# One core: FFN gate and up as one Winograd-Strassen block product, the hidden activation split in the down stage

## The chip, the cores and the metric

The kernel runs on one core of a Trainium2 chip. The metric is the device time of one execution in microseconds (us); the times below are of three runs, and the profile is of one execution more.

## The reference

One transformer-like block over 512 tokens of width 1024: layer norm 0, an input projection, a gated-MLP branch and an HGRN2 branch, a gated merge, an output projection with layer norm 1, a feed-forward part with a per-layer-embedding (PLE) gate, and layer norm 2. What the change touches, with `D_FF` = 2816:

```python
mix = jnp.einsum("bsd,de->bse", merged, w_o[i])
h1 = _layer_norm(ALPHA * h + mix, ln1_g[i], ln1_b[i])
hid = jax.nn.silu(jnp.einsum("bsd,df->bsf", h1, w_ffn_gate[i])) * jnp.einsum("bsd,df->bsf", h1, w_ffn_up[i])
ffn = jnp.einsum("bsf,fd->bsd", hid, w_ffn_down[i])
ple = (jax.nn.sigmoid(jnp.einsum("bsd,de->bse", h1, w_ple_gate[i]) + b_ple_gate[i])
       * jnp.einsum("bsr,rd->bsd", p[i], w_ple[i]))
h = _layer_norm(ALPHA * h1 + ffn + ple, ln2_g[i], ln2_b[i])
```

All inputs are float32, and the result is held to float32 accuracy.

## The kernel before, in words

Every large product is done in float32r from operands that are split in two: `split` (L59) makes the high part h with a cast on ACT (L61) and the low part l with a subtraction (L64), on DVE unless `eng` names another engine. A product is then three matmuls per tile: h by h, h by l, l by h. Weights come from DRAM in units of 512 KB through `load_unit` (L66): SP issues the transfer into a `raw` tile (three buffers), ACT and DVE make `wh` and `wl` (five buffers each).

`gemm_a` (L84) puts features on partitions: the 128x128 weight tile is stationary and the activation, 512 tokens, streams; 48 matmuls with 512 columns for 256 features over K = 1024. `mm_b` (L96) puts tokens on partitions.

The stages are written one after another: PLE product and layer norm 0, HGRN2 by pairs of heads, gated MLP, merge, output projection with layer norm 1 (`ps_wo`; tiles `r1`, `h1h`, `h1l`), PLE gate (`ps_pg`), then the FFN. `turn` (L696) transposes a normed token tile on PE and splits it into `h1h` and `h1l`, straight from PSUM. In the PLE gate a token tile's result goes DVE (add bias, `sgp`), ACT (sigmoid), POOL (times `pl`), DVE (into `r1`).

The FFN loop (L740 on) runs over 11 units m of 256 hidden features. Each unit is two `gemm_a`, `fg` (gate) and `fu` (up), so 96 matmuls and four weight units. Then ACT takes silu from PSUM, DVE multiplies (`fhf`, L753), and `split` makes `hidh` and `hidl` at once. The down stage (`ps_d`) runs over 11 pairs of hidden tiles, and ends with layer norm 2 and the stores.

A scheduler sets the order of each engine's queue when the program is built, from this text and its own estimates; each engine works its queue in that order. Tiles live in pools. A tile placed where an earlier pool lay may be written when the earlier tiles there are done with, and such a wait can stand on any queue, SP's included. PSUM has four tiles of two banks (`ps_tile`).

Of the kernel before, what the change touches and what calls it, by code (L numbers as in the profile page):

```python
# [31 lines left out]
def block_kernel(  # L32
# [155 lines left out]
    with tc.tile_pool(name="start", bufs=1) as sp:  # L188
# [188 lines left out]
    def keys(m, psf):  # L377
        """forget gates, their products, decayed keys"""
# [31 lines left out]
        fl = lambda ap: ap.rearrange("p g c -> p (g c)")  # noqa: E731  # L410
# [56 lines left out]
    def scores(m):  # L467
        """scores, [s, t] of each block of 128 tokens; states at the starts of blocks 1..3"""
# [33 lines left out]
    def outputs(m):  # L502
        """tokens on partitions, normed"""
# [56 lines left out]
    # =============== gated MLP: v, normed; the last pair of heads beside it ===============  # L560
# [13 lines left out]
    # blocks of 64 positions: a later one is not seen from an earlier one  # L574
# [62 lines left out]
    # =============== merge ===============  # L637
# [22 lines left out]
    # =============== output projection, layer norm 1, PLE gate ===============  # L660
# [4 lines left out]
    h1h = h1pool.tile([P, KT, T], F32R, name="h1h")  # L665
    h1l = h1pool.tile([P, KT, T], F32R, name="h1l")
    with tc.tile_pool(name="l1", bufs=1) as lp:
# [4 lines left out]
        g1 = load_bc(lp, ln1_g[0], "g1")  # L672
        b1 = load_bc(lp, ln1_b[0], "b1")
        bpg = load_bc(lp, b_ple_gate[0], "bpg")
        # the residual: alpha * layer norm 0
        for t in range(TT):
# [3 lines left out]
            V.scalar_tensor_tensor(out=r1[:, t, :], in0=xr, scalar=mr0[:, t, 1:2], in1=b0a, op0=ALU.mult, op1=ALU.add)  # L680
        acc = [ps_tile(f"ps_wo{t}") for t in range(TT)]
# [14 lines left out]
        def turn(t):  # L696
# [20 lines left out]
        yapool_cm.__exit__(None, None, None)  # L717
        for c in range(2):
# [20 lines left out]
    # =============== FFN ===============  # L739
    with tc.tile_pool(name="hid", bufs=1, side="right") as fp:  # L740
        hidh = fp.tile([P, FT, T], F32R, name="hidh")
        hidl = fp.tile([P, FT, T], F32R, name="hidl")
        for m in range(FT // 2):
            psg = ps_tile(f"ps_fg{m}")
            gemm_a(psg, wg, 256 * m, h1h, h1l, f"fg{m}")
            psu = ps_tile(f"ps_fu{m}")
            gemm_a(psu, wu, 256 * m, h1h, h1l, f"fu{m}")
            for a in range(2):
                f = 2 * m + a
                sg = fp.tile([P, T], F32, tag="fsg", name=f"fsg{f}", bufs=2)  # L750
                S.activation(sg, psg[:, a, :], AF.Silu)
                hf = fp.tile([P, T], F32, tag="fhf", name=f"fhf{f}", bufs=2)
                V.tensor_tensor(out=hf, in0=psu[:, a, :], in1=sg, op=ALU.mult)  # L753
                split(hidh[:, f, :], hidl[:, f, :], hf)
        h1pool_cm.__exit__(None, None, None)

        with tc.tile_pool(name="fin", bufs=1) as lp:
# [15 lines left out]
            tails = [(kp, [unit_b(wd, 2 * kp, 512 * c, f"d{kp}_{c}", pool=lp, bufs=4) for c in range(2)])  # L773
                     for kp in range(NP - TAIL, NP)]
            for t in range(TT):
# [52 lines left out]
```

## Time and profile before

| | |
|---|---|
| median of 3 runs | 997.42 us (996.73 to 997.47) |
| span of the profiled execution, first to last instruction | 992.0 us |
| output projection's wait to first gate matmul | about 571 to 577 us |
| PLE gate | about 577 to 623.5 us |
| FFN gate and up, first `ps_fg` to first `ps_d` | 623.54 to 862.90 us |
| down stage, layer norm 2, stores | 862.90 to 992.0 us |

PE is the matmul engine, PEld its weight load, DVE the vector engine, ACT the scalar engine, POOL the GpSimd, SP the engine that issues transfers. [...] A wait belongs to the instruction that stood still; the chain follows the work that ended last back to its start.

### The profile page before, as it was taken

The page shows a single profiled execution, that of the slowest core. Times are in us where ns is not written, and L with a number is a line of the kernel's source. Part 1 is how long each engine was busy: PE and PEld are TensorE (multiplying, and loading weights), DVE is VectorE, ACT ScalarE, POOL GpSimd, SP SyncE. Part 2 cuts the span into 40 slices and gives each one's busy share as a digit, 9 for nine tenths or more (in the row PEclk, how much of TensorE's full clock was granted, in tenths as well). Part 3 has the DMA queues.
Part 4 walks back from the last instruction along what each step waited for, and adds up shares of the span by engine and source line. Part 5 has one row for each costly group of instructions (what it writes and reads, how often), then busy time and mean ns, then how long its engine had stood idle before and what let it go on. Part 6 is the DMA issues. An engine that isn't in the chain of part 4 may idle for free.

```text
span 992.0 us, 11393 instructions
## 1 busy us (share of the span) xinstructions
PE 963.9 (97%) x4745; PEld 795.3 (80%) x4745; DVE 474.0 (48%) x538; ACT 289.6 (29%) x335; POOL 132.0 (13%) x106
## 2 busy tenths in 40 slices
PE   6999999998999999999999989999999999999996
PEld 5788878787888888888888868888888888888885
DVE  6667935767249543332324984333323333311307
ACT  4244222333324332232322222332223223212301
POOL 5314410505006000000000332000000000000004
PEclk9999999999999999999999999999999999999999
DMA  8343223225222423333235425333332333322302
GB/s 288 127 138 107 65 81 90 64 65 167 66 65 85 128 77 94 95 97 102 89 106 216 166 81 153 98 93 103 89 106 87 104 90 101 132 102 85 128 1 85
DMA packets 79939, 104.60 MB, mean 105 GB/s; under 512 B 3368, under 2 KB 60304, under 8 KB 79888
## 3 DMA queue, kind: packets, MB, share of 16 engines
q1 hardware_dynamic: 79888, 103.88, 33.4%
q8 instruction: 37, 0.61, 0.3%
q14 instruction: 14, 0.11, 0.0%
HBM read 99.67 MB, written 4.19 MB: 105 GB/s over the span
## 4 chain that ended last, share of the span: by engine, by line
PE 84%; DVE 9%; POOL 2%; DMA 2%; issue 1%; ACT 1%; SPq 0%; DVEq 0%; ACTq 0%; POOLq 0%
PE ps_fu L93 4%; PE ps_fg L93 4%; PE ps_fg L94 4%; PE ps_fu L94 4%; PE ps_fg L92 4%; PE ps_fu L92 4%; PE ps_d L99 4%; PE ps_d L98 4%; PE ps_d L100 4%; PE ps_pg L99 2%; PE ps_pg L98 2%; PE ps_pg L100 2%; PE ps_mwa L93 2%; PE ps_mwa L92 2%; PE ps_mwa L94 2%; PE ps_f L92 1%
## 5 line engine op out<-in xcount | busy, mean ns | idle before, releaser
L64 DVE TENSOR_TENSOR wl_fu<-raw_fu,wh_fu 128x1024 fp32r<-128x1024 f32 x22 | 27.0, 1225 | 88.3 <-ACT wh_fu L61 88.3
L92 PE MATMUL ps_fg<-h1h,wh_fg 128*128 128x512 f32 x176 | 68.5, 389 | 0.0
L93 PE MATMUL ps_fg<-h1l,wh_fg 128*128 128x512 f32 x176 | 68.5, 389 | 0.0
L94 PE MATMUL ps_fg<-h1h,wl_fg 128*128 128x512 f32 x176 | 68.5, 389 | 0.0
L92 PE MATMUL ps_fu<-h1h,wh_fu 128*128 128x512 f32 x176 | 68.5, 389 | 0.0
L93 PE MATMUL ps_fu<-h1l,wh_fu 128*128 128x512 f32 x176 | 68.5, 389 | 0.0
L94 PE MATMUL ps_fu<-h1h,wl_fu 128*128 128x512 f32 x176 | 68.5, 389 | 0.0
L99 PE MATMUL ps_d<-wl_d,hidh 128*128 128x512 f32 x172 | 67.8, 394 | 0.0
L98 PE MATMUL ps_d<-wh_d,hidh 128*128 128x512 f32 x172 | 67.4, 392 | 0.0
L100 PE MATMUL ps_d<-wh_d,hidl 128*128 128x512 f32 x172 | 66.7, 388 | 0.0
L139 POOL TENSOR_TENSOR mr<-mr,nhalf 128x1 f32<-128x1 f32 x12 | 12.1, 1043 | 365.7 <-DVE mr L138 365.7
L64 DVE TENSOR_TENSOR wl_d<-raw_d,wh_d 128x1024 fp32r<-128x1024 f32 x22 | 26.8, 1224 | 67.1 <-ACT wh_d L61 66.9
L61 ACT CAST wh_fu<-raw_fu 128x1024 fp32r<-128x1024 f32 x22 | 23.2, 1054 | 82.8 <-PE ps_fg L93 43.9
L61 ACT CAST wh_d<-raw_d 128x1024 fp32r<-128x1024 f32 x22 | 23.0, 1052 | 79.2 <-PE ps_d L100 52.4
L61 ACT CAST wh_fg<-raw_fg 128x1024 fp32r<-128x1024 f32 x22 | 23.2, 1055 | 75.6 <-PE ps_fu L93 39.8
L64 DVE TENSOR_TENSOR wl_fg<-raw_fg,wh_fg 128x1024 fp32r<-128x1024 f32 x22 | 26.9, 1220 | 27.4 <-ACT wh_fg L61 27.4
L64 POOL TENSOR_TENSOR wl_pg<-raw_pg,wh_pg 128x1024 fp32r<-128x1024 f32 x3 | 8.0, 2671 | 231.8 <-ACT wh_pg L61 231.8
L92 PEld LDWEIGHTS ps_fu<-h1h,wh_fu 128*128 128x128 f32 x176 | 33.0, 188 | 6.9
L92 PEld LDWEIGHTS ps_fg<-h1h,wh_fg 128*128 128x128 f32 x176 | 33.0, 188 | 6.9
L93 PEld LDWEIGHTS ps_fg<-h1l,wh_fg 128*128 128x128 f32 x176 | 33.0, 188 | 6.9
L93 PEld LDWEIGHTS ps_fu<-h1l,wh_fu 128*128 128x128 f32 x176 | 33.0, 188 | 6.9
L94 PEld LDWEIGHTS ps_fg<-h1h,wl_fg 128*128 128x128 f32 x176 | 33.0, 188 | 6.8
(283 smaller groups left out, 2408.6 us busy)
## 6 DMA issues: line engine op xcount, KB each, us to landing
raw_fg<-in_w_ffn_gate_dram SPq DMA_DIRECT2D x22, 512.0 KB, 3.8
raw_fu<-in_w_ffn_up_dram SPq DMA_DIRECT2D x22, 512.0 KB, 3.8
raw_d<-in_w_ffn_down_dram SPq DMA_DIRECT2D x22, 512.0 KB, 3.2
raw_i<-in_w_in_dram SPq DMA_DIRECT2D x8, 512.0 KB, 5.7
raw_f<-in_w_in_dram SPq DMA_DIRECT2D x8, 512.0 KB
raw_q<-in_w_in_dram SPq DMA_DIRECT2D x8, 512.0 KB, 3.8
raw_g<-in_w_in_dram SPq DMA_DIRECT2D x8, 512.0 KB, 4.1
raw_v<-in_w_in_dram SPq DMA_DIRECT2D x8, 512.0 KB, 3.8
```

The source lines that it names most:

```text
L61: S.copy(h, src)
L64: (eng or V).tensor_tensor(out=l, in0=src, in1=h.bitcast(F32), op=ALU.subtract)
L92: PE.matmul(ps[:, j, :], h[:, k, cs], acth[:, kk, :], start=first, stop=False)
L93: PE.matmul(ps[:, j, :], h[:, k, cs], actl[:, kk, :], start=False, stop=False)
L94: PE.matmul(ps[:, j, :], l[:, k, cs], acth[:, kk, :], start=False, stop=last)
L98: PE.matmul(ps, acth[:, kk, ts], h[:, k, :], start=first, stop=False)
L99: PE.matmul(ps, acth[:, kk, ts], l[:, k, :], start=False, stop=False)
L100: PE.matmul(ps, actl[:, kk, ts], h[:, k, :], start=False, stop=last)
L139: G.tensor_tensor(out=dst, in0=dst, in1=nhalf[:, 0:n], op=ALU.pow)
```

## The change

The gate and up weights stand side by side as one matrix, W11 and W12 (first half of K, gate and up), W21 and W22 (second half). The activation is cut in halves of the tokens and of K. A Winograd form of Strassen's scheme then takes seven products of half size for eight. Per unit of 256 features a product is 24 matmuls with 256 columns, 168 in all, where 96 with 512 columns stood.

- The activation's sums are made once, in `combine`, in the PLE gate at t = 3: four subtractions, five splits. For them `turn` first copies the transposed tile to `h1f` (float32) on ACT and splits from there.
- The weights' sums t1 to t4 are made for every unit by POOL, four additions of 128x1024. Each of the seven weight operands is split by ACT and DVE.
- Two PSUM tiles are used per unit: X and Z in one, Y in the other. Products are accumulated on top of each other; ACT copies X once (`p1`) and DVE takes `y6`, `z5` and three results `fq` from PSUM, then two products into `hid`.
- `raw` tiles of w_up (`raw_*_01`, `raw_*_11`) lie in the FFN's own pool `up`, not in `wpool`. The residual gets a pool of its own, `res`, ahead of the pool of layer norm 1 and the gate.
- `hid` is kept as one float32 tile; the split into `hidh` and `hidl` is done by pairs in the down stage.

```diff
+    def combine(pool, scratch, f, first):
+        a11, a12 = f[:, 0:4, 0:HT], f[:, 4:8, 0:HT]
+        a21, a22 = f[:, 0:4, HT:T], f[:, 4:8, HT:T]
...
+        for n, x, y in (("s1", a21, a22), ("a6", a11, raw["s1"]), ("a7", a21, a11), ("a3", a12, raw["a6"])):
+            V.tensor_tensor(out=raw[n], in0=x, in1=y, op=ALU.subtract)
+        for n in ("a6", "s1", "a7", "a3"):
+            split(*c[n], raw[n])
+        S.activation(c["22"][0], a22, AF.Copy, scale=-1.0)
+        V.scalar_tensor_tensor(out=c["22"][1], in0=a22, scalar=-1.0, in1=c["22"][0].bitcast(F32),
+                               op0=ALU.mult, op1=ALU.subtract)
+        return c
+    def product_a(bank, w, a, first, last):
+        h, l = w
+        ah, al = a
+        for j in range(2):
+            o = bank[:, HT * j:HT * j + HT]
+            cs = slice(j * P, (j + 1) * P)
+            for k in range(4):
+                PE.matmul(o, h[:, k, cs], ah[:, k, :], start=first and j == 0 and k == 0, stop=False,
...
+    def winograd_a(pool, src, comb, name, done):
+        raw = {}
+        for a, b in ((0, 0), (0, 1), (1, 1), (1, 0)):
+            w, k0, c0 = src[a][b]
+            raw[a, b] = (pool if b else wpool).tile([P, 4, 256], F32, tag="raw", name=f"raw_{name}_{a}{b}", bufs=3)
...
+            G.tensor_tensor(out=t, in0=x, in1=y, op=ALU.add)
...
+        product_a(X, parts("11", raw[0, 0]), comb["11"], True, False)
+        S.copy(p1, xv3)
+        t1 = add("t1", raw[0, 0], raw[0, 1])
+        t2 = add("t2", t1, raw[1, 1])
+        product_a(Y, parts("t2", t2), comb["a6"], True, False)
+        V.tensor_tensor(out=y6, in0=yv3, in1=p1, op=ALU.subtract)
+        product_a(Z, parts("t1", t1), comb["s1"], True, False)
+        V.tensor_tensor(out=z5, in0=zv3, in1=p1, op=ALU.subtract)
+        product_a(X, parts("21", raw[1, 0]), comb["12"], False, True)
+        done(0, 0, xv3, None, False)
+        t3 = add("t3", raw[0, 1], raw[1, 1])
+        product_a(Y, parts("t3", t3), comb["a7"], False, False)
+        done(1, 1, yv3, z5, False)
+        product_a(Z, parts("22", raw[1, 1]), comb["a3"], False, True)
+        done(0, 1, zv3, y6, False)
+        t4 = add("t4", t2, raw[1, 0])
+        product_a(Y, parts("t4", t4), comb["22"], False, True)
+        done(1, 0, yv3, p1, True)
...
-            split(h1h[:, :, ts], h1l[:, :, ts], psv)
...
+            f = h1f[:, :, t * P:(t + 1) * P]
+            S.copy(f, psv)
+            split(h[:, :, ts], l[:, :, ts], f)
...
+                if c == 0 and t == 3:
+                    comb = combine(cpool, h2pool, h1f, (h1h, h1l))
...
-            psg = ps_tile(f"ps_fg{m}")
-            gemm_a(psg, wg, 256 * m, h1h, h1l, f"fg{m}")
-            psu = ps_tile(f"ps_fu{m}")
-            gemm_a(psu, wu, 256 * m, h1h, h1l, f"fu{m}")
...
+            winograd_a(fp, [[(w, 4 * kh, 256 * m) for w in (wg, wu)] for kh in range(2)], comb, f"f{m}", done)
...
+            def hid_pair(kp):
+                h = lp.tile([P, 2, T], F32R, tag="hidh", name=f"hidh{kp}", bufs=4)
+                l = lp.tile([P, 2, T], F32R, tag="hidl", name=f"hidl{kp}", bufs=4)
+                split(h, l, hid[:, 2 * kp:2 * kp + 2, :])
+                return h, l
```

On DVE, one FFN unit of the kernel before stands like this in its queue (`wl` are the splits' low parts):

```order
L753 TENSOR_TENSOR fhf6_4896<-ps_fu3_4833,fsg6_4894 128x512
L753 TENSOR_TENSOR fhf7_4902<-ps_fu3_4833,fsg7_4900 128x512
L64 TENSOR_TENSOR wl_fg5_0_5044<-raw_fg5_0_5041,wh_fg5_0_5043 128x1024
L64 TENSOR_TENSOR hidl_4369<-fhf6_4896,hidh_4368 128x512
L64 TENSOR_TENSOR hidl_4369<-fhf7_4902,hidh_4368 128x512
L64 TENSOR_TENSOR wl_fg5_1_5074<-raw_fg5_1_5071,wh_fg5_1_5073 128x1024
L64 TENSOR_TENSOR wl_fu5_0_5105<-raw_fu5_0_5102,wh_fu5_0_5104 128x1024
L64 TENSOR_TENSOR wl_fu5_1_5135<-raw_fu5_1_5132,wh_fu5_1_5134 128x1024
```

In the changed kernel the first FFN unit, f0, stands like this on DVE (wl_f0_t2 is the low part of sum t2; wl_f1_11 already belongs to the next unit):

```order
L840 SCALAR_TENSOR_TENSOR r1_3689<-r1_3689,sgp1_3_4402 128x512
L65 TENSOR_TENSOR wl_f0_t2_4467<-t2_f0_4464,wh_f0_t2_4466 128x1024
L65 TENSOR_TENSOR wl_f0_t1_4496<-t1_f0_4462,wh_f0_t1_4495 128x1024
L65 TENSOR_TENSOR wl_f0_21_4525<-raw_f0_10_4426,wh_f0_21_4524 128x1024
L65 TENSOR_TENSOR wl_f0_t3_4556<-t3_f0_4553,wh_f0_t3_4555 128x1024
L65 TENSOR_TENSOR wl_f0_22_4586<-raw_f0_11_4424,wh_f0_22_4585 128x1024
L194 TENSOR_TENSOR y6_f0_4431<-ps_f0_y_4429,p1_f0_4430 128x512
L65 TENSOR_TENSOR wl_f0_t4_4619<-t4_f0_4616,wh_f0_t4_4618 128x1024
L196 TENSOR_TENSOR z5_f0_4432<-ps_f0_xz_4428,p1_f0_4430 128x512
L65 TENSOR_TENSOR wl_f1_11_4666<-raw_f1_00_4652,wh_f1_11_4665 128x1024
L867 TENSOR_TENSOR fq0_11_4583<-ps_f0_y_4429,z5_f0_4432 128x512
```

Reads from PSUM that free a bank for the next product (y6, z5, fq) now stand among the splits; before, PSUM was read only after a unit's end.

On SP, the first weight transfers of the FFN in the kernel before, all into `wpool`, pass between the last transfers `pl` of the gate:

```order
L69 DMA raw_fg0_0_4371<-in_w_ffn_gate_dram 128x4x256
L732 DMA pl0_3_4206<-ple_dram_84 128x512
L69 DMA raw_fg0_1_4401<-in_w_ffn_gate_dram 128x4x256
L732 DMA pl1_0_4262<-ple_dram_84 128x512
L69 DMA raw_fu0_0_4432<-in_w_ffn_up_dram 128x4x256
L69 DMA raw_fu0_1_4462<-in_w_ffn_up_dram 128x4x256
```

And in the changed kernel:

```order
L169 DMA raw_f0_10_4426<-in_w_ffn_gate_dram 128x4x256
L169 DMA raw_f1_00_4652<-in_w_ffn_gate_dram 128x4x256
L836 DMA pl1_1_4339<-ple_dram_84 128x512
L836 DMA pl1_2_4371<-ple_dram_84 128x512
L836 DMA pl1_3_4403<-ple_dram_84 128x512
L169 DMA raw_f0_01_4422<-in_w_ffn_up_dram 128x4x256
L169 DMA raw_f0_11_4424<-in_w_ffn_up_dram 128x4x256
L169 DMA raw_f1_01_4654<-in_w_ffn_up_dram 128x4x256
```

The two `raw` tiles of w_up moved behind every `pl`; raw_f0_01 lies where the gate's pool lay, and its transfer waits for the gate's last update of `r1` (the row `r1_3689<-r1_3689,sgp1_3_4402` of DVE above).

The end of the FFN on DVE in the changed kernel (hid holds the product, hidl0 is the first split of the down stage):

```order
L867 TENSOR_TENSOR fq10_01_6933<-ps_f10_xz_6748,y6_f10_6751 128x512
L865 TENSOR_TENSOR fq10_10_6966<-p1_f10_6750,ps_f10_y_6749 128x512
L872 TENSOR_TENSOR hid_4414<-fq10_01_6933,fsg10_0_6738 128x2x256
L65 TENSOR_TENSOR wl_d2_0_7114<-raw_d2_0_7111,wh_d2_0_7113 128x1024
L872 TENSOR_TENSOR hid_4414<-fq10_11_6903,fsg10_1_6739 128x2x256
L65 TENSOR_TENSOR hidl0_6996<-hid_4414,hidh0_6995 128x1024
```

The cast hidh0 on ACT stands in the place of pools that the FFN used, and waits for the second `hid` row; the first matmul of `ps_d` waits for hidh0. Before, hidden tiles 0 and 1 had been split ten units earlier.

## Rows read from the trace of the kernel before

**Rows 1.** Page, first part: busy us (share of the span) xinstructions by engine.
```profile
PE 963.9 (97%) x4745; PEld 795.3 (80%) x4745; DVE 474.0 (48%) x538; ACT 289.6 (29%) x335; POOL 132.0 (13%) x106
```
**Rows 2.** Waits of PE from 500 us on: waited for, us, times, longest.
```profile
PE ps_h L700 <- DVE r L159: 3.7, 1, 3.7
```
**Rows 3.** Stretches: us, busy us of PE, PEld, DVE, ACT, POOL, PEclk, DMA, GB/s.
```profile
571.00:575.00 4.00, 0.35 (x2) 0.00 (x0) 4.00 (x5) 0.00 (x0) 2.88 (x2) 0.95 0.01 4
575.00:578.00 3.00, 2.98 (x11) 2.45 (x12) 2.96 (x5) 0.97 (x2) 1.46 (x1) 0.50 0.49 169
578.00:625.00 47.00, 47.00 (x213) 38.42 (x213) 28.72 (x35) 15.43 (x19) 10.99 (x8) 1.00 0.38 112
625.00:864.00 239.00, 239.00 (x1056) 197.97 (x1055) 79.74 (x88) 69.99 (x89) 1.47 (x1) 1.00 0.34 99
```
**Rows 4.** Timeline of PE at both ends of the FFN: start us, us, line.
```profile
623.54 0.39 PE L92 MATMUL ps_fg<-h1h,wh_fg 128*128 128x512 f32 x1
623.77 0.39 PE L93 MATMUL ps_fg<-h1l,wh_fg 128*128 128x512 f32 x1
...
862.68 0.39 PE L94 MATMUL ps_fu<-h1h,wl_fu 128*128 128x512 f32 x1
862.90 0.39 PE L98 MATMUL ps_d<-wh_d,hidh 128*128 128x512 f32 x1
```
**Rows 5.** Timeline of PE and PEld around the last spatial-gate products.
```profile
347.35 3.73 PE L614 MATMUL ps_mx<-wsT,vn 128*128 128x128 f32 x32
350.83 0.48 PE L92 MATMUL ps_mga<-hh,wh_ga 128*128 128x512 f32 x1
...
347.12 3.76 PEld L614 LDWEIGHTS ps_mx<-wsT,vn 128*128 128x128 f32 x32
```
**Rows 6.** Groups by line and form: xcount, busy us, mean ns of one, idle before.
```profile
L92 PEld LDWEIGHTS ps_fg<-h1h,wh_fg 128*128 128x128 f32 x176 | 33.0, 188 | 6.9
...
L614 PEld LDWEIGHTS ps_mx<-wsT,vn 128*128 128x128 f32 x64 | 7.6, 192 | 0.2
```
**Rows 7.** Timeline of POOL and of DVE, 311 to 323 us.
```profile
311.56 2.40 POOL L157 TENSOR_TENSOR vn<-vn,gmb 128x1024 f32<-128x1024 f32 x1
...
315.42 5.75 POOL L157 TENSOR_TENSOR vn<-vn,gmb 128x1024 f32<-128x1024 f32 x2
...
311.83 3.22 DVE L154 SCALAR_TENSOR_TENSOR vn<-vn,mrv,gmg 128x1024 f32<-128x1024 f32 x1
...
316.29 2.62 DVE L64 TENSOR_TENSOR wl_gu<-raw_gu,wh_gu 128x1024 fp32r<-128x1024 f32 x1
318.83 3.42 DVE L64 TENSOR_TENSOR ybl<-gt,ybh 128x1024 fp32r<-128x1024 f32 x1
```
**Rows 8.** Timeline of DVE and of POOL, 591 to 594 us.
```profile
591.55 1.23 DVE L64 TENSOR_TENSOR h1l<-ps_h,h1h 128x1024 fp32r<-128x1024 f32 x1 [1.10 <-ACT h1h L61]
...
592.12 1.30 POOL L735 TENSOR_TENSOR sgp<-sgp,pl 128x512 f32<-128x512 f32 x1 [5.09 <-ACT sgp L734]
```
**Rows 9.** Groups of DVE and ACT in the FFN, as in rows 6.
```profile
L64 DVE TENSOR_TENSOR wl_fg<-raw_fg,wh_fg 128x1024 fp32r<-128x1024 f32 x20 | 24.4, 1221 | 26.2 <-ACT wh_fg L61 26.2
L753 DVE TENSOR_TENSOR fhf<-ps_fu,fsg 128x512 f32<-128x512 f32 x22 | 14.2, 686 | 36.9 <-PE ps_fu L94 36.9
L64 DVE TENSOR_TENSOR hidl<-fhf,hidh 128x512 fp32r<-128x512 f32 x20 | 12.9, 684 | 0.0
...
L61 ACT CAST wh_fg<-raw_fg 128x1024 fp32r<-128x1024 f32 x22 | 23.2, 1055 | 75.6 <-PE ps_fu L93 39.8
```
**Rows 10.** Timeline of DVE, the gate's last tile; transfers by line: KB each, us to landing.
```profile
624.66 0.68 DVE L733 TENSOR_TENSOR sgp<-ps_pg,bpg 128x512 f32<-128x512 f32 x1
...
627.65 0.69 DVE L736 SCALAR_TENSOR_TENSOR r<-r,sgp 128x512 f32<-128x512 f32 x1 [1.18 <-POOL sgp L735]
...
raw_fu<-in_w_ffn_up_dram SPq DMA_DIRECT2D x22, 512.0 KB, 3.8
```

More of the change, by code (lines that the diff above doesn't have):

```diff
@@ L19 @@
 TT = T // P
+HT = T // 2
 DFF = 2816
@@ new lines, in product_a @@
+    def product_a(bank, w, a, first, last):
[6 more added lines that the diff above has]
+                PE.matmul(o, h[:, k, cs], ah[:, k, :], start=first and j == 0 and k == 0, stop=False,
+                          skip_group_check=True)
+                PE.matmul(o, h[:, k, cs], al[:, k, :], start=False, stop=False, skip_group_check=True)
+                PE.matmul(o, l[:, k, cs], ah[:, k, :], start=False, stop=last and j == 1 and k == 3,
+                          skip_group_check=True)
@@ new lines, in winograd_a, with add, parts, mid @@
+    def winograd_a(pool, src, comb, name, done):
[3 more added lines that the diff above has]
+            raw[a, b] = (pool if b else wpool).tile([P, 4, 256], F32, tag="raw", name=f"raw_{name}_{a}{b}", bufs=3)
+            nc.sync.dma_start(raw[a, b], w[k0 * P:(k0 + 4) * P, c0:c0 + 256].rearrange("(k p) c -> p k c", p=P))
+        def add(n, x, y):
+            t = pool.tile([P, 4, 256], F32, tag="wt", name=f"{n}_{name}", bufs=4)
+            G.tensor_tensor(out=t, in0=x, in1=y, op=ALU.add)
+            return t
+        def parts(n, x):
+            h = wpool.tile([P, 4, 256], F32R, tag="wh", name=f"wh_{name}_{n}", bufs=5)
+            l = wpool.tile([P, 4, 256], F32R, tag="wl", name=f"wl_{name}_{n}", bufs=5)
+            split(h, l, x)
+            return h, l
+        def mid(n, bufs=1):
+            return pool.tile([P, 2, HT], F32, tag=n, name=f"{n}_{name}", bufs=bufs)
+        psa, psb = ps_tile(f"ps_{name}_xz"), ps_tile(f"ps_{name}_y")
+        X, Z, Y = psa[:, 0, :], psa[:, 1, :], psb[:, 0, :]
+        xv3, yv3, zv3 = (z.rearrange("p (a c) -> p a c", c=HT) for z in (X, Y, Z))
+        p1, y6, z5 = mid("p1", 2), mid("y6"), mid("z5")
+        product_a(X, parts("11", raw[0, 0]), comb["11"], True, False)
[16 more added lines that the diff above has]
+        done(1, 0, yv3, p1, True)
@@ L664, in block_kernel @@
     h1pool = h1pool_cm.__enter__()
-    h1h = h1pool.tile([P, KT, T], F32R, name="h1h")
-    h1l = h1pool.tile([P, KT, T], F32R, name="h1l")
-    with tc.tile_pool(name="l1", bufs=1) as lp:
+    h1h = h1pool.tile([P, KT, HT], F32R, name="h1h")
+    h1l = h1pool.tile([P, KT, HT], F32R, name="h1l")
+    with tc.tile_pool(name="res", bufs=1) as lp:
         g0a = load_bc(lp, ln0_g, "g0a")
@@ L707, in block_kernel @@
             if t > 1:
+                if t == 2:
+                    h1f = lp.tile([P, KT, T], F32, name="h1f")
                 turn(t - 2)
@@ L737, in block_kernel, with silu, done @@
                                        op0=ALU.mult, op1=ALU.add)
-    with tc.tile_pool(name="hid", bufs=1, side="right") as fp:
-        hidh = fp.tile([P, FT, T], F32R, name="hidh")
-        hidl = fp.tile([P, FT, T], F32R, name="hidl")
-        for m in range(FT // 2):
-            psg = ps_tile(f"ps_fg{m}")
-            gemm_a(psg, wg, 256 * m, h1h, h1l, f"fg{m}")
-            psu = ps_tile(f"ps_fu{m}")
-            gemm_a(psu, wu, 256 * m, h1h, h1l, f"fu{m}")
[L748 to L755, printed above, removed]
+        h2pool_cm.__exit__(None, None, None)
+    fpool_cm = tc.tile_pool(name="hid", bufs=1, side="right")
+    fpool = fpool_cm.__enter__()
+    hid = fpool.tile([P, FT, T], F32, name="hid")
+    with tc.tile_pool(name="up", bufs=1) as fp:
+        for m in range(FT // 2):
+            hv = [hid[:, 2 * m:2 * m + 2, HT * i:HT * i + HT] for i in range(2)]
+            sgs = [fp.tile([P, 2, HT], F32, tag="fsg", name=f"fsg{m}_{i}", bufs=2) for i in range(2)]
+            def silu(i, src):
+                S.activation(sgs[i], src, AF.Silu)
+            def done(i, j, src, add, sub):
+                if j == 0 and add is None:
+                    silu(i, src)
+                    return
+                o = fp.tile([P, 2, HT], F32, tag="fq", name=f"fq{m}_{i}{j}", bufs=3)
+                if sub:
+                    V.tensor_tensor(out=o, in0=add, in1=src, op=ALU.subtract)
+                else:
+                    V.tensor_tensor(out=o, in0=src, in1=add, op=ALU.add)
+                if j == 0:
+                    silu(i, o)
+                ups[i, j] = o
+                if (i, 1) in ups and (i == 0 or (1, 0) in ups):
+                    V.tensor_tensor(out=hv[i], in0=ups[i, 1], in1=sgs[i], op=ALU.mult)
+            ups = {}
+            winograd_a(fp, [[(w, 4 * kh, 256 * m) for w in (wg, wu)] for kh in range(2)], comb, f"f{m}", done)
+    h1pool_cm.__exit__(None, None, None)
+    if True:
         with tc.tile_pool(name="fin", bufs=1) as lp:
```

35 lines of the change are left out of this document (25 added, 10 removed).

## Prediction

> **What bounds the kernel now.** I read the engines' line of the page first: PE is busy 97% of the span, DVE 48%, ACT 29%, POOL 13% [rows 1]. So the time is PE's time, and the waits of PE say where it is not. From 500 us on there is one, 3.7 us before the first transposes of the gate stage [rows 2]. [...] The FFN is the plainest stretch of the kernel: 239.00 of 239.00 us busy on PE with 1056 matmuls. Its timeline runs from 623.54 to 862.90, so one matmul of 512 columns costs 239.36/1056 = 226.7 ns, one unit of 96 costs 21.76 us, and the down stage follows without a gap [rows 4]. DVE is busy 79.74 of those 239 us, ACT 69.99, POOL 1.47 [rows 3]: nearly idle, which is the room that the change spends.
>
> **What one small matmul costs.** The change puts 168 matmuls of 256 columns in the place of 96 of 512. No matmul of 256 columns stands in the trace. Half of 226.7 is 113.3 ns. The nearest row that is shorter is `ps_mx`: 32 matmuls of 128 columns begin at 347.35 and the next product at 350.83, so 3.48/32 = 109 ns each [rows 5]. That row also shows that 109 ns is sustained while each matmul loads weights of its own: the 32 loads have records of 192 ns, as long as the FFN's 188 [rows 6], and overlap. Outer bounds are 188 ns (one load record after another) and 226.7 (no gain per column). I take 113.3, nearest to the `ps_mx` row; 109 to 120 is its own spread, the 120 if part of the 226.7 doesn't shrink with the columns. A unit is then 168 x 113.3 = 19.0 us against 21.76. The unit breaks even at 21.76/168 = 129.5 ns.
>
> [...]
>
> **What the rest costs: POOL and DVE against each other.** Per unit POOL gets four adds of 128x1024, two inputs in SBUF. One takes 2.40 us alone. The timelines of 311 to 323 us show what happens when DVE has a two-input SBUF operation at the same time [rows 7]. POOL begins 315.42; its first operation would end at 317.82. The split `wl_gu` begins 316.29 and ends 318.91, 1.09 after that, although a split takes 1.22 in the FFN [rows 9]. POOL's second then ends at 321.17, 2.26 after 318.91, and `ybl` at 322.25, 1.08 later. They exclude each other, and a pair costs 2.26 + 1.08 = 3.34. Operations of DVE that read PSUM are spared: `h1l` from `ps_h` takes 1.23 with POOL running beside it [rows 8].
>
> Of one unit under this exclusion: four adds, seven weight splits and two `hid` products. Contested: 4 x 2.26 + 7 x 1.08 + 2 x 0.62 (0.69 [rows 9] less the same tenth) = 17.8 us; at the lone durations 4 x 2.40 + 7 x 1.22 + 2 x 0.69 = 19.5. PE's 19.0 lies between. So DVE and POOL together have become as long as PE, though each alone looks half idle.
>
> **The change part by part.**
>
> (a) *Gate stage.* Nine operations of `combine` on DVE, 9 x 1.22 = 11.0 us; on ACT four copies to `h1f` and five casts, 9 x 1.05 = 9.5 [rows 9]. DVE is busy 28.72 of 47.00 us there and ACT 15.43 [rows 3], so both fit. But the splits of the gate's next weight units stand in DVE's queue behind most of the nine, and with POOL active beside them; I take a PE wait of some 3 us. The first turns get a copy of 1.05 us ahead of their split; the residual loaded earlier may give back part of the 3.7 [rows 2]. Net **+3** (-2, if all of that comes back and the splits are early enough, to +9, most of the nine uncovered).
>
> (b) *First unit.* `raw_f0_01` lies where the gate's pool lay, so SP issues it after the gate's last update of `r1`; `raw_f0_11` and the next units' w_up stand behind it on SP. In the trace of before that tail is 624.66 to 628.34, 3.7 us after the last gate matmul, and a unit takes 3.8 us to land [rows 10]. Then t1 2.40 and t2 2.40 on POOL, one cast 1.05: 3.7 + 3.8 + 2.4 + 2.4 + 1.05 = 13.4. Product 11 needs only `wpool` and hides 24 x 0.1133 = 2.7: PE idles 10.6. After that `y6` stands behind five splits in DVE's queue, and Y may not be added to before `y6` is read. POOL catches up on its adds at the same time, so the five go at 3.34 a pair: 5 x 3.34 + 0.7 = 17.4, while PE has three products, 8.2: another 9. **+19.6** (10.6, if splits aren't held up, to 24).
>
> (c) *Steady units.* PE's 19.0, plus what the queue adds: product t4 may not begin before `fq_11` has read Y, and `fq_11` stands behind a split of the next unit. If an add holds that split, 2.26 + 1.08 + 0.68 = 4.0 against one product, 2.7: 1.3 late. An add runs in half of the time (9.0 of 19.0), which is 0.65, and 17.8 of 19.0 leaves hardly room to catch up: I take 0.9 between 0.65 and 1.3. Unit 19.9, 11 x (19.9 - 21.76) = **-20.5** (-24 at 109 ns, where the port's 17.8 to 19.5 paces the unit; -8.8 at 120 ns, 21.0 a unit).
>
> (d) *To the down stage.* After the last matmul: `fq10_10` 0.69, `hid` 0.69, split `wl_d2_0` 1.22, `hid` 0.69, cast `hidh0` 1.05 [rows 9], 4.3, and four passes from engine to engine: **+5** (3 to 7). Before, nothing waited there. The other hidden splits keep ahead: the down stage has DVE free, and one pair is two operations.
>
> (e) *Clock.* After a 3.7 us wait the trace has 3 us at half clock [rows 3], which loses 1.5 us. Counted once for the wait in b: **+1.5** (0 to 3).
>
> Sum: 3 + 19.6 - 20.5 + 5 + 1.5 = **+8.6**. On the span of 992.0 that is 1000.6; the median stands 5.4 above that span, so **1006.0 us**.
>
> **The rivals.**
>
> *R1, the exclusion doesn't reach PE: faster.* Splits run ahead by their five buffers, adds by their four, so single holds are smoothed; PE keeps 19.0 a unit, b is only its 10.6, a +1. 1 + 10.6 - 30.4 + 5 + 1.5 = -12.3: **985 us**. For it: 17.8 is under 19.0, and PSUM reads are free. Against: the order puts PSUM reads between splits, and the first unit starts with nothing made ahead. It decides once the mean unit is under about 19.2 us.
>
> *R2, the small matmul costs more than its columns.* At 130 ns the FFN gains nothing and b, a, d, e stay: about 1028; at 188 ns, one load record each, 11 x (31.6 - 21.76) = +108 and b to e on top, about **1126 us**. For it: the records of loads are longer than 113 ns. Against: `ps_mx`.
>
> *R3, even.* At 109 ns and b of about 15: 3 + 15 - 24 + 5 + 1 = 0: **997 us**.
>
> *R4, it does not do what it says.* A part of the seven products' saving could be missing if matmuls were added elsewhere; the count, 1848 for 1056, all others unchanged, excludes that.
>
> **How the numbers follow.** A change of 0.2%, 2 us, is about what a measurement of this kernel can tell from none. The forecast, slower, mostly 1000 to 1019 (b at 24 and a at 9 against 15 and 0): 0.60. R1 0.20. R3 0.10. R2 0.10. Faster 0.20, same 0.10, slower 0.70. The range reaches from R1's 985 (half of R1 below it) to 1026, which leaves out most of R2: 985 to 1026.
>
> **What would show it.** In the changed kernel's profile: (1) matmul starts in one product 113 ns apart; above 130 the forecast's sign stands but by R2. (2) POOL near 4 x 2.3 us a unit, and splits of the FFN with records well over 1.22 us, ending about 1.08 after an add's end; if their mean stays 1.22, R1. (3) A PE wait of 8 to 13 us at the second product of unit f0, for a cast of t2, and waits at its t3 product for `y6`. (4) First product to first product 19.9 us in later units. (5) A wait of 4 to 6 us before the first `ps_d`. (6) PEclk 0.50 behind the wait of (3). The forecast is wrong if waits (3) are small, because the order of the queues lets units be made ahead, or if the pitch is off by more than 5 ns, since each 1 ns is 1.85 us.

## The result and the profile after

The changed kernel takes 1008.18 us (median; 1007.03 to 1009.97) against 997.08 of the kernel before: 1.0123 times, 95% interval 1.0098 to 1.0149, so 1.2% slower. The forecast was 1006.0. Its profiled execution spans 1005.3 us, 13.3 more than before.

The engines' line of the page, beside [rows 1]: PE has 16 us less to do and a smaller share of a longer span; DVE has 142 us more, POOL 124.

```profile
PE 947.9 (94%) x5537; PEld 816.5 (81%) x5537; DVE 615.6 (61%) x624; ACT 337.0 (34%) x377; POOL 256.3 (25%) x150
```

The waits of PE from 500 us on (waited for, us in all, times, longest). Where [rows 2] had one wait of 3.7, there are now these:

```profile
PE ps_f_y L156 <- ACT wh_f_t L62: 10.8, 1, 10.8
PE ps_f_y L156 <- DVE y_f L194: 9.3, 10, 4.3
PE ps_d L99 <- issue: 4.8, 1, 4.8
PE ps_pg L101 <- DVE h2l L65: 2.5, 2, 2.2
PE ps_pg L101 <- DVE h1l L65: 2.3, 1, 2.3
PE ps_pg L100 <- DVE wl_pg L65: 1.4, 1, 1.4
PE ps_wo L100 <- DVE wl_wo L65: 1.0, 1, 1.0
```

Two rows of 0.6 and 0.2 us, in the first FFN unit, are left out.

The stretches, in the columns of [rows 3] (PEclk is the granted TensorE clock as a share of full speed): gate stage, first FFN unit, the other ten, the way to the down stage.

```profile
573.00:627.40 54.40, 48.27 (x218) 38.40 (x217) 40.70 (x47) 19.92 (x23) 17.15 (x9) 1.00 0.25 78
627.40:665.54 38.14, 22.30 (x148) 21.32 (x147) 25.35 (x14) 12.13 (x13) 25.98 (x10) 0.78 0.40 118
665.54:867.50 201.96, 196.96 (x1690) 195.19 (x1689) 176.43 (x141) 89.65 (x101) 96.83 (x36) 1.00 0.33 99
867.50:881.00 13.50, 8.66 (x34) 7.01 (x33) 9.48 (x10) 5.58 (x7) 0.00 (x0) 0.75 0.52 191
```

POOL is at work in 97 of the 202 us of the steady units, DVE in 176 (it had 80 of 239 in [rows 3]), and PE has gaps there for the first time. Cut at the same places, the two spans differ like this:

| stretch, us | before | after | difference | forecast |
|---|---|---|---|---|
| start to last matmul of the output projection | 570.97 | 573.02 | +2.05 | a: +3 with the next row |
| from there to the first FFN matmul | 52.57 | 54.38 | +1.81 | |
| FFN, first matmul to end of the last | 239.36 | 241.82 | +2.46 | b, c, e: +0.6 |
| gap before the down stage | 0 | 4.84 | +4.84 | d: +5 |
| down stage to the end | 129.10 | 131.24 | +2.14 | 0 |
| sum | 992.0 | 1005.3 | +13.3 | +8.6 |

**How one wait comes about.** Each steady unit looks the same to the hundredth of a microsecond. Below: the wait of PE in four units in a row, then DVE and POOL in the last of them (start us, us, engine, line, out<-in; in brackets the idle time before, and what ended it).

```profile
676.94 0.39 PE L156 MATMUL ps_f_y<-ca7h,wh_f_t 128*128 128x256 f32 x1 [0.56 <-DVE y_f L194]
...
697.14 0.39 PE L156 MATMUL ps_f_y<-ca7h,wh_f_t 128*128 128x256 f32 x1 [0.56 <-DVE y_f L194]
...
717.34 0.39 PE L156 MATMUL ps_f_y<-ca7h,wh_f_t 128*128 128x256 f32 x1 [0.56 <-DVE y_f L194]
...
737.54 0.39 PE L156 MATMUL ps_f_y<-ca7h,wh_f_t 128*128 128x256 f32 x1 [0.56 <-DVE y_f L194]
```
```profile
732.84 0.69 DVE L872 TENSOR_TENSOR hid<-fq,fsg 128x512 f32<-128x512 f32 x1
733.44 3.44 DVE L65 TENSOR_TENSOR wl_f<-raw_f,wh_f 128x1024 fp32r<-128x1024 f32 x1
736.81 0.68 DVE L194 TENSOR_TENSOR y_f<-ps_f_y,p_f 128x512 f32<-128x512 f32 x1
```
```profile
733.00 2.79 POOL L173 TENSOR_TENSOR t_f<-raw_f,raw_f 128x1024 f32<-128x1024 f32 x1 [2.17 <-DVE wl_f_t L65]
```

The unit is 20.20 us long. POOL's add t3 runs from 733.00 to 735.79. The split of operand 22 is given to DVE at 733.44 and ends at 736.88, 1.09 after the add, as in [rows 7]: 3.44 us where [rows 9] had 1.22. `y6` stands behind it and ends at 737.49, and PE's product t3 begins at 737.54. Over the whole FFN the groups show the same (count, busy us, mean ns):

```profile
L65 DVE TENSOR_TENSOR wl_f<-raw_f,wh_f 128x1024 fp32r<-128x1024 f32 x32 | 80.1, 2504 | 3.9 <-ACT wh_f L62 3.9
L65 DVE TENSOR_TENSOR wl_f_t<-t_f,wh_f_t 128x1024 fp32r<-128x1024 f32 x44 | 76.2, 1733 | 14.5 <-ACT wh_f_t L62 14.4
```

### The profile page after: what moved, and what is told of

It is laid out like the page before. It is cut to its first block, busy times and chain, and to the rows that moved or that the text cites. A ratio compares the mean times of both kernels' runs of the same rounds, so it can differ in the third digit from the quotient of the medians.

```text
span 1005.3 us, 13248 instructions
## 1 busy us (share of the span) xinstructions
PE 947.9 (94%) x5537; PEld 816.5 (81%) x5537; DVE 615.6 (61%) x624; ACT 337.0 (34%) x377; POOL 256.3 (25%) x150
## 4 chain that ended last, share of the span: by engine, by line
PE 68%; DVE 15%; issue 6%; DMA 5%; POOL 3%; ACT 2%; SPq 1%; DVEq 0%; POOLq 0%; ACTq 0%
PE ps_d L99 4%; PE ps_d L100 4%; PE ps_d L101 4%; PE ps_f_xz L156 3%; PE ps_f_xz L159 3%; PE ps_f_xz L158 3%; PE ps_f_y L156 2%; PE ps_f_y L159 2%; PE ps_f_y L158 2%; DVE wl_f L65 2%; PE ps_v L99 2%; PE ps_v L100 1%; PE ps_mwa L94 1%; PE ps_v L101 1%; PE ps_mwa L95 1%
## 5 line engine op out<-in xcount | busy, mean ns | idle before, releaser
L65 DVE TENSOR_TENSOR wl_f<-raw_f,wh_f 128x1024 fp32r<-128x1024 f32 x41 | 91.6, 2233 | 18.6 <-ACT wh_f L62 18.6
L65 DVE TENSOR_TENSOR wl_f_t<-t_f,wh_f_t 128x1024 fp32r<-128x1024 f32 x44 | 76.2, 1733 | 14.5 <-ACT wh_f_t L62 14.4
L62 ACT CAST wh_f_t<-t_f 128x1024 fp32r<-128x1024 f32 x44 | 46.1, 1051 | 94.8 <-PE ps_f_xz L158 42.8
L173 POOL TENSOR_TENSOR t_f<-raw_f,raw_f 128x1024 f32<-128x1024 f32 x22 | 59.1, 2688 | 52.2 <-DVE wl_f_t L65 47.2
L173 POOL TENSOR_TENSOR t_f<-t_f,raw_f 128x1024 f32<-128x1024 f32 x22 | 62.5, 2840 | 38.0 <-issue 36.3
L62 ACT CAST wh_f<-raw_f 128x1024 fp32r<-128x1024 f32 x41 | 42.9, 1046 | 56.7 <-PE ps_f_xz L158 16.2
L156 PE MATMUL ps_f_xz<-h1h,wh_f 128*128 128x256 f32 x176 | 49.6, 282 | 0.0
L159 PE MATMUL ps_f_xz<-h1h,wl_f 128*128 128x256 f32 x176 | 49.6, 282 | 0.0
L158 PE MATMUL ps_f_xz<-h1l,wh_f 128*128 128x256 f32 x176 | 49.5, 281 | 0.0
L99 PEld LDWEIGHTS ps_d<-wh_d,hidh 128*128 128x128 f32 x172 | 33.1, 193 | 12.1 <-issue 5.0
L156 PE MATMUL ps_f_y<-ca6h,wh_f_t 128*128 128x256 f32 x88 | 25.7, 292 | 10.8 <-ACT wh_f_t L62 10.8
```

The source lines that it names most:

```text
L62: S.copy(h, src)
L65: (eng or V).tensor_tensor(out=l, in0=src, in1=h.bitcast(F32), op=ALU.subtract)
L99: PE.matmul(ps, acth[:, kk, ts], h[:, k, :], start=first, stop=False)
L156: PE.matmul(o, h[:, k, cs], ah[:, k, :], start=first and j == 0 and k == 0, stop=False, skip_group_check=True)
L158: PE.matmul(o, h[:, k, cs], al[:, k, :], start=False, stop=False, skip_group_check=True)
L159: PE.matmul(o, l[:, k, cs], ah[:, k, :], start=False, stop=last and j == 1 and k == 3, skip_group_check=True)
```

## The experiments

All are edits of the changed kernel. Experiments 1 to 7 and 10 were run once each, 8 and 9 four times. Stretches are compared from their own first instruction, since what stands ahead of the gate stage ended up to 2.5 us apart where its code is the same. The gate stage itself, from the last matmul of the output projection to the first of the FFN, took 54.4 to 55.9 us in the six profiles with the same gate code (the changed kernel and experiments 1, 2, 4, 5 and 6).

**1. Without the additions.** The theory was that POOL's adds and DVE's splits exclude each other and that this reaches PE; the rival, that `y6` simply stands behind too much on DVE.

```diff
-            t = pool.tile([P, 4, 256], F32, tag="wt", name=f"{n}_{name}", bufs=4)
-            G.tensor_tensor(out=t, in0=x, in1=y, op=ALU.add)
-            return t
+            return y
```

> Leaves out the four additions of POOL: each of t1 to t4 is one of its two terms, so the FFN computes something else. DVE's queue stands in the steady units as in the changed kernel, row for row. Theory (POOL's adds and DVE's splits exclude each other, and the stretched split ahead of y6 makes PE wait): splits fall to 1.22 us, the unit from 20.20 to 19.4 us, the first unit's wait for y6 from 4.3 us to nothing, its wait for the cast of t2 from 10.8 to 6.0 (two adds of 2.4 less); span about 985 us. Rival (y6 stands behind five splits, and that alone costs, adds or none): the unit stays at 20.2 and the first wait for y6 at 4.3; only the 4.8 of the two adds comes back, span about 1000 us.

Span 986.1. The splits take 1.22 again, no wait for `y6` is left, and the unit (two starts of the same matmul) is 679.59 - 660.23 = 19.36 us:

```profile
660.23 0.29 PE L156 MATMUL ps_f_y<-ca6h,wh_f_t 128*128 128x256 f32 x1
...
679.59 0.29 PE L156 MATMUL ps_f_y<-ca6h,wh_f_t 128*128 128x256 f32 x1
```
```profile
L65 DVE TENSOR_TENSOR wl_f_t<-raw_f,wh_f_t 128x1024 fp32r<-128x1024 f32 x34 | 41.6, 1224 | 15.8 <-ACT wh_f_t L62 15.2
L65 DVE TENSOR_TENSOR wl_f<-raw_f,wh_f 128x1024 fp32r<-128x1024 f32 x25 | 30.6, 1223 | 18.0 <-ACT wh_f L62 18.0
```

With DVE's queue in the same order the wait is gone, so the order alone does not make it. The first unit's wait for the cast of t2 fell to 7.4, less than the two adds say (6.0 was expected).

**2. One pair of rows exchanged.**

```diff
-        V.tensor_tensor(out=y6, in0=yv3, in1=p1, op=ALU.subtract)
+        y6_i = V.tensor_tensor(out=y6, in0=yv3, in1=p1, op=ALU.subtract)
...
-        product_a(Z, parts("22", raw[1, 1]), comb["a3"], False, True)
+        with tc.issue_after(y6_i.ins):
+            w22 = parts("22", raw[1, 1])
+        product_a(Z, w22, comb["a3"], False, True)
```

> One edit: in DVE's queue y6 stands ahead of the split of operand 22 instead of behind it, everything else in the steady units as before. Theory (only the one stretched split of 3.4 us ahead of y6 reaches PE): no wait for y6, unit 20.20 to 19.4 us, span 1005.3 less some 9 to 10 = 996 us. Rival (DVE and POOL together, 17.8 to 19.5 us a unit, are the bound): the wait moves to z5 or fq or to a late split, the unit stays at 20.0 to 20.2, span 1003 or more.

Span 1003.1, unit 20.04 to 20.14: the rival. The wait moved to `fq_11`:

```profile
719.05 2.41 POOL L173 TENSOR_TENSOR t_f<-t_f,raw_f 128x1024 f32<-128x1024 f32 x1 [3.55 <-issue]
```
```profile
719.44 3.10 DVE L65 TENSOR_TENSOR wl_f<-raw_f,wh_f 128x1024 fp32r<-128x1024 f32 x1
722.47 0.68 DVE L869 TENSOR_TENSOR fq<-ps_f_y,z_f 128x512 f32<-128x512 f32 x1
```
```profile
723.20 0.39 PE L156 MATMUL ps_f_y<-c22h,wh_f_t 128*128 128x256 f32 x1 [0.21 <-DVE fq L869]
```

The next add, at 719.05, holds the next split, and behind that stands the read that product t4 needs. An exchange in the queue only chooses which read is late.

**3. The first unit stocked beside the gate.** The tiles that the gate's second half needs moved to another pool, so that one pool with w_up's `raw` tiles and the sums opens after its first half:

```diff
+            if c == 0:
+                l1_cm.__exit__(None, None, None)
+                fa_cm = tc.tile_pool(name="fa", bufs=1)
+                fa = fa_cm.__enter__()
...
-            raw[a, b] = (pool if b else wpool).tile([P, 4, 256], F32, tag="raw", name=f"raw_{name}_{a}{b}", bufs=3)
+            raw[a, b] = (fa if b else wpool).tile([P, 4, 256], F32, tag="raw", name=f"raw_{name}_{a}{b}", bufs=3)
```

> Only places in SBUF change: the raw tiles of w_up and the sums t lie in a pool of their own which opens when the first half of the gate stage is done; what the gate's second half needs (gate weights, sgp, pl, bias) lies elsewhere. Theory (the first unit waits for the gate's pool, then for a transfer and two adds in a row, and starts with nothing made ahead): transfers and adds run beside the gate's second half, the waits of 10.8 and 4.3 us go, the first unit takes about 20 instead of 38.1 us, span about 987 us. Rival (the adds then exclude the gate's own splits, so the waits appear in the gate): the gate grows by 5 us or more and the span stays above 995 us.

Span 989.1, FFN and gap 237.45 us instead of 246.66. The wait for the cast of t2 is gone and the gate is not longer (51.69 us to 54.38), so its rival falls. Of the 16.2 us that the span is shorter, 3.6 lie ahead of the gate stage, where nothing that the theory names was changed. And 8.4 us came back at another place:

```profile
PE ps_f_xz L156 <- ACT p_f L190: 8.4, 1, 8.4
PE ps_f_y L156 <- DVE y_f L194: 4.9, 9, 0.5
```

`p1` still lay in the late pool, whose place the gate's last update of `r1` frees. The theory of the place was right; one tile had been left out of the repair. The steady waits stay, as they must.

**4. The first hidden pair in the weights' pool.**

```diff
+                if kp == 0:
+                    h = wpool.tile([P, 2, T], F32R, tag="wh", name=f"hidh{kp}", bufs=5)
+                    l = wpool.tile([P, 2, T], F32R, tag="wl", name=f"hidl{kp}", bufs=5)
```

> One edit: the two split tiles of the first pair of hidden tiles lie in the weights' pool instead of where the FFN's pool lay. Theory (the first cast of the down stage waits for the place alone, since its hidden tiles were done ten units before): the wait of 4.84 us before the down stage falls under 1 us, and so does the half clock behind it; span 1005.3 less 6 to 7 = 999 us. Rival (splits of the down weights, queued behind the last hid products, are late as well): a wait of 2.5 us or more stays, span above 1002 us.

Span 998.7. The row for `ps_d` is gone from PE's waits, and the first four `ps_d` even stand ahead of the FFN's last product. So the whole way is compared: from the first FFN matmul to the end it is 370.4 us instead of 377.9, 7.5 less. The gap came from that place (the scheduler also gave PE's queue this new order).

**5. The additions on DVE.** The strictest test of the exclusion: the work stays, and the busier engine gets it.

```diff
-            G.tensor_tensor(out=t, in0=x, in1=y, op=ALU.add)
+            V.tensor_tensor(out=t, in0=x, in1=y, op=ALU.add)
```

> One edit: the four additions t1 to t4 of each unit are made by DVE instead of POOL; the result stays the same. Theory (POOL's adds and DVE's splits exclude each other, so that giving work to POOL takes more from DVE than it saves): with POOL idle an add takes 1.22 us on DVE, splits take 1.22 again, and DVE's unit is 11 x 1.22 + 7 x 0.69 = 18.3 us, under PE's 19.4; unit 19.4 to 19.6 us, first unit shorter by at least 2 x 1.2; span about 993 us. Rival (DVE is simply short of time and needs POOL's help): DVE becomes the bound at 18.3 us of work in a row with waits for casts in it, unit 20.5 us or more, span 1008 us or more.

Span 994.5, unit 685.36 - 665.68 = 19.68 us. DVE is busy 164.60 of 195 us there, with four adds a unit more, and less than the 176.43 of 202 that it had with POOL's help; POOL is idle. PE has no wait in the steady units; that they take 19.68 and not the 19.36 of experiment 1 is slower matmuls (see the last section).

```profile
665.00:860.00 195.00, 194.55 (x1662) 194.35 (x1660) 164.60 (x176) 88.55 (x102) 0.00 (x0) 1.00 0.36 103
```
```profile
L65 DVE TENSOR_TENSOR wl_f<-raw_f,wh_f 128x1024 fp32r<-128x1024 f32 x29 | 35.2, 1215 | 0.0
L173 DVE TENSOR_TENSOR t_f<-t_f,raw_f 128x1024 f32<-128x1024 f32 x17 | 20.7, 1220 | 0.3
```

**6. One streamed operand for all products.**

```diff
-        product_a(Y, parts("t2", t2), comb["a6"], True, False)
+        product_a(Y, parts("t2", t2), comb["11"], True, False)
```

and so for the other five.

> All seven products stream the same activation operand (the first quarter, in h1h and h1l) instead of the combinations, so the FFN computes something else; order, banks and sizes stay. In the changed kernel products 11 and 21, which stream h1h and h1l and write bank X, take 119.5 ns a matmul, the other five 113.6. Theory (it is the place of the streamed tiles): all seven take 119.5 ns, 20.1 us of PE in a unit. Rival (it is the bank written): only the products on X take 119.5, as before. Span within 5 us of the changed kernel's either way, since a slower PE hides some of the waits for y6.

In the changed kernel product t1 needs 676.11 - 673.50 = 2.61 us for 23 steps, 113.5 ns each; the stretch of product 21 that streams h1h and h1l, 682.88 - 679.78 = 3.10 us for 26, 119.2.

```profile
673.50 0.28 PE L156 MATMUL ps_f_xz<-cs1h,wh_f_t 128*128 128x256 f32 x1
...
676.11 0.28 PE L159 MATMUL ps_f_xz<-cs1h,wl_f_t 128*128 128x256 f32 x1
```

With one operand t1 has 120.0 (699.87 - 697.11 = 2.76 for 23):

```profile
697.11 0.28 PE L156 MATMUL ps_f_xz<-h1h,wh_f_t 128*128 128x256 f32 x1
...
699.87 0.28 PE L159 MATMUL ps_f_xz<-h1h,wl_f_t 128*128 128x256 f32 x1
```

So here it goes with the streamed tile, not with the bank: t1 writes the same bank Z in both. (The tile alone doesn't settle it; see the last section.) The span was 1016.4, 11 us longer, not within 5: the unit became 21.2 us, because a slower PE did not hide the waits for `y6` (0.8 in most units here).

**7. Turn straight from PSUM.**

```diff
-            S.copy(f, psv)
-            split(h[:, :, ts], l[:, :, ts], f)
+            split(h[:, :, ts], l[:, :, ts], psv)
+            S.copy(f, psv)
```

> One edit in the gate stage: turn splits the transposed tile straight from PSUM, as in the kernel before, and copies it to h1f afterwards for the combinations. Theory (the copy of 1.05 us ahead of each split, and the split then reading two SBUF tensors, make the gate's waits of 2.3 us for h1l and of 2.2 to 2.5 for h2l): both waits go or fall under 1 us, span 1005.3 less 3 to 5 = 1001 us. Rival (the waits come from what stands ahead in DVE's queue): they stay within 0.5 us of what they were.

Span 1006.3. The wait for h1l fell from 2.3 to 0.7 us and those for h2l went, but the one for `wl_pg` behind them grew from 1.4 to 3.5 (that for `wl_wo` was there before, 1.0 too):

```profile
PE ps_pg L100 <- DVE wl_pg L65: 3.5, 1, 3.5
PE ps_wo L100 <- DVE wl_wo L65: 1.0, 1, 1.0
PE ps_pg L101 <- DVE h1l L65: 0.7, 1, 0.7
```

From the last output projection matmul to the FFN it is 53.92 us, against 54.4 to 55.9 without the edit: 0.5 to 1.9 of the 3 to 5 us expected. The span shows nothing of it, because the output projection ended 3.0 us later in this execution, some 2.6 of them from waits in the first 300 us, which the edit does not touch. Neither expectation fits: the copy does cause the two waits, but most of what they cost came back in the wait for `wl_pg`. What sets that one was not tried.

**8. All repairs together.** Experiments 3 (with p1, y6 and z5 in the early pool), 4, 5 and 7.

> All repairs together: additions on DVE, the first unit's transfers and sums made beside the gate's second half (with p1, y6 and z5 in the early pool too), the first hidden pair in the weights' pool, turn straight from PSUM. Theory (every microsecond lost is one of these waits): FFN 11 x 19.4 = 213 us, gate as long as in the kernel before, no gap at the end; 992.0 - 239.4 + 213 + some 5 for what is left = 971 us span, 2% under the kernel before. Rival (the load moved to DVE in the gate and the FFN makes new waits): above 985 us.

971.17 us, 0.9748 times the kernel before (95% interval 0.9708 to 0.9788). Two waits from 500 us on:

```profile
PE ps_f_xz L156 <- ACT p_f L190: 6.1, 1, 6.1
PE ps_pg L100 <- DVE wl_pg L65: 1.2, 1, 1.2
```

Steady units take 19.36 us. The profiled span, 971.6, meets the expectation by two parts that the theory did not have: the first unit's wait and the half clock behind it (t1's matmuls begin 213.6 ns apart, 638.52 - 633.82 = 4.70 us for 22) cost 6.1 + 2.6 us, and from the last output projection matmul to the FFN it is 48.68 us, 3.9 less than in the kernel before. The 6.1 is the first unit's. DVE had fallen behind with the additions, the first of which waited 4.24 us for its transfer, and took the bias add of the gate's last tile at 630.57, 9 us after that tile's last matmul; so the last sigmoid was late, and `p1` stood behind it on ACT.

**9. The same with the first unit's additions held back behind the gate's bias adds.** `sg_i` holds the gate's bias adds by half and tile:

```diff
-        t1 = add("t1", raw[0, 0], raw[0, 1])
-        t2 = add("t2", t1, raw[1, 1])
+        with (tc.issue_after(after[0].ins) if after else ExitStack()):
+            t1 = add("t1", raw[0, 0], raw[0, 1])
+            t2 = add("t2", t1, raw[1, 1])
...
+            winograd_a(fa, fp, ..., (sg_i[1, 1], sg_i[1, 3]) if m == 0 else None)
```

> All repairs together, and in DVE's queue the first unit's additions t1, t2 stand behind the gate's second bias add and t3, t4 behind its last one. In c2_all the bias add of the gate's last tile stood behind additions that waited for a transfer, so the last sigmoid and, behind it on ACT, the copy p1 were late, and PE waited 6.1 us, then ran 2.6 us longer at half clock. Theory: both go, span 971.6 less 8 = 963 us. Rival (the additions come later now, and the cast of t2 is late in their place): a wait of 4 us or more at the first t2 product, span 968 or more.

972.23 us, 0.9761 (0.9744 to 0.9777): no different from experiment 8, so the theory's 963 was missed; the time is the rival's, but its wait at the t2 product is 0.8 us and not 4. The 6.1 went, but 1.7 for `y6`, 0.8 for the cast of t2 and 2.6 instead of 1.2 for `wl_pg` came. The units from the third on take 19.68 us instead of 19.36 with no wait in them, as in experiment 5, some 2.5 us in all. From the first FFN matmul to the first `ps_d` the profile is 3 us shorter (216.08 to 219.21), and the medians don't show it.

**10. Experiment 8 with the additions back on POOL.**

> The kernel c2_all with one thing taken back: the additions t1 to t4 are made by POOL again. Theory (the exclusion costs in every unit, whatever the start): units of 20.2 us with a wait for y6 of some 0.5 in each, span c2_all's 971.6 plus 9 to 12 = 982 us. Rival (only the unstocked start made the exclusion reach PE): units of 19.4, span 972 to 975 us.

Span 985.5, 14 us above experiment 8. The unit is 684.74 - 664.55 = 20.19 us again. So a well stocked start does not smooth the exclusion away.

```profile
PE ps_f_xz L156 <- ACT p_f L190: 7.6, 1, 7.6
PE ps_f_y L156 <- DVE y_f L194: 7.1, 10, 2.2
```

## Why the prediction was right, and where its terms were off

- **The small matmul.** 113.3 ns was taken; five products have 113.5 and the two on h1h and h1l 119.2. R2 fell. PE's part of the unit is 19.36 us, not 19.0, by experiment 1.
- **(c) steady units.** 20.20 us against 19.9: the queue's share is 0.84 (0.9 taken), the rest is the slower pair of products. 11 x (20.20 - 21.76) = -17.2, forecast -20.5. The mechanism was the one named, shown by experiments 1, 5 and 10; its place was not: the late read was `y6` behind the split of 22. `fq_11`, which the forecast named, is late only once `y6` is not (experiment 2). That a port sets the pace, as the forecast words it, no run shows; the runs show the times, 3.44 us for a split that meets an add and 1.22 for one that meets none (experiment 1).
- **(b) first unit and (e) clock.** Together 241.82 - 11 x 20.20 = +19.6; forecast 19.6 + 1.5 = 21.1. But the two parts were both off. The idle time was 10.8 for the cast of t2, 0.7 for its next steps and 4.3 for `y6`: 15.9, not 19.6; of the five splits ahead of `y6` the last two went at the pace forecast (3.42 and 3.37 for 3.34), but the first two took 5.61 together and one 1.21, since fewer of them met an add. (15.9 of idle time and 4.9 for the clock, less twice the regular wait of 0.84 that the 20.20 counts for the first and the last unit too, give 19.1 of the 19.6.)
- **(e) was the term mis-sized most.** It was counted once, at 1.5. In the profiled execution the granted clock fell after three waits, of 10.8, 4.3 and 4.8 us, to a mean of 0.51, 0.64 and 0.55 in the stretches behind them:

```profile
641.20:648.30 7.10, 6.32 (x26) 5.73 (x27) 7.07 (x4) 3.78 (x4) 5.94 (x3) 0.51 0.27 74
...
655.30:659.60 4.30, 4.25 (x25) 4.28 (x26) 4.30 (x3) 0.00 (x0) 3.08 (x2) 0.64 0.46 126
```
```profile
874.06:881.00 6.94, 6.94 (x18) 5.45 (x19) 4.57 (x4) 2.75 (x3) 0.00 (x0) 0.55 0.55 212
```

  The first cost 7.06 - 0.73 of waits - 26 x 0.1135 = 3.4 us, the second 4.23 - 2.72 = 1.5, the third 15 matmuls in 6.38 us instead of 3.4: 3.0. That is 7.9 us, of which 4.9 fall into the first unit and 3.0 into the down stage, for which the forecast had nothing. A wait did not always bring the fall: behind the 2.3 us for h1l the granted clock stayed at 1.00 here, while with the same gate code it fell there in experiments 1, 2, 4 and 5 (0.57 from 576 to 580 us in experiment 2; in experiment 5 matmuls of 512 columns begin 427 ns apart, 581.86 - 578.87 = 2.99 us for 7), and the gate took 55.8 to 55.9 us instead of 54.4.
- **(d)** 4.84 for 5, and the chain was the one counted, with one `fq` more at its head, 0.61 us. That four passes from engine to engine cost 0.7 was an estimate that no row gave; the one from the end of `hid`, 872.20 + 0.69, to the cast at 872.92 is 0.03. Experiment 4 shows that the place of one pool made it.
- **(a)** +1.8 in the gate itself, within its range (up to +3.3 in the other profiles with its code); the 2.05 us ahead of it are no more than the spread of what stands there. The waits for h1l and `wl_pg` were named, that for h2l was not.
- **The base, and luck.** The sum gave +8.6 on the span and +13.3 was measured; the time missed by only 2.2 us, because another step failed the other way. The 5.4 us between span and median were taken for time outside the span. For the changed kernel it is 1007.04 - 1005.3 = 1.7; if it was the same before, the profiled execution there took some 993.7 us, a quick one among runs of 992.4 to 998.4. A step of 3.7 us hid a shortfall of 4.7; the other 1.1 or so is the median's distance from the profiled run. The mechanisms are the ones forecast; that the time came so close is luck.
- **R1** gave 985 us for a kernel in which the exclusion does not reach PE, a span of 992.0 - 12.3 = 979.7. Experiment 1, where there is no exclusion, took 987.82 us with a span of 986.1. The times are close only by the same 3.7 us of the base: on the span R1 was 6.4 us too low, although experiment 1 also saves the first unit's two adds, which R1 still paid. R1 lost on its condition, and its price was too low as well.

## What to carry to other kernels

Before giving work to an idle engine, look in the trace for what its operations do to the neighbour's: here an add on POOL took 2.34 us with DVE idle and 2.79 beside a split, that split took 3.44 instead of 1.22, and DVE itself made an add in 1.22 (experiment 5), so that the help cost more than it gave. A saving inside a loop has to survive its first and its last round: look which pool place, transfer and queue position the first operand waits for, and add what the clock may cost behind a wait, 1.5 to 3.4 us for each of 4 to 11 us here. With these mended the kernel of experiment 8 gains 2.5%; before, the change was a loss. Not all of it is the seven products for eight: of the 20.4 us between the profiled spans, 18.4 stand behind the first FFN matmul and 3.9 in the gate, and 1.9 were lost ahead of it.

## What the runs showed of the hardware that was not expected

The time of a matmul was not set by its columns alone here. With weights, columns, order and bank the same, t1's took 113.5 ns from the tiles of the combinations and 120.0 from h1h and h1l (experiment 6); the 120 ns that the forecast held as an upper end was the value for h1h and h1l. But the same tiles did not always give the same time. In experiment 5, at a granted clock of 1.00 and without a wait, t1 took 710.34 - 707.63 = 2.71 us for 23 steps, 117.8 ns each, from the tile that gave 113.5 in the changed kernel:

```profile
707.63 0.28 PE L156 MATMUL ps_f_xz<-cs1h,wh_f_t 128*128 128x256 f32 x1
...
710.34 0.28 PE L159 MATMUL ps_f_xz<-cs1h,wl_f_t 128*128 128x256 f32 x1
```

The products on ca6 (707.51 - 705.04 = 2.47 us for 21 steps, 117.6) and ca7 (713.17 - 710.46 = 2.71 for 23, 117.8) were as slow there, and all three again in experiment 9 (117.6 to 117.8), while those on c22 and ca3 stayed near 113.5 (on ca3 723.01 - 720.40 = 2.61 for 23); this makes the unit of 19.68 us. In both runs PE's queue has another order (two matmuls on ca6 stand far ahead of the others), in experiment 8, with the additions on DVE too, it has not, and its units take 19.36. Whether the order is the cause, and which property of a tile makes the 6.5 ns of experiment 6, was not tried and stays open.
